# Second-layer softmax: the reciprocal row sums go through DRAM and scale the head outputs, instead of scaling the probabilities

## Chip, cores and metric

The kernel runs on one core of one Trainium2 chip. The metric is device time in microseconds; smaller is better. Before the change the median of three runs is 756.14 us (754.92 to 758.21).

## The reference

Two layers over 512 latent tokens and 256 context tokens with 1024 features. The first layer uses differential attention, the second grouped-query attention with 8 query heads of 128, 2 key/value heads and a gate path. What matters here is the second layer's mixer:

```python
def sweep_attention(q, k, v):
    ...
        s = jnp.einsum('bqhgd,bkhd->bhgqk', qblk.astype(jnp.float32), k32) * scale
        p = jax.nn.softmax(s, axis=-1)
        return jnp.einsum('bhgqk,bkhd->bqhgd', p.astype(v.dtype), v)
    ...

def gqa_mixer(h, hc, w_in, w_out, qk_g, cos, sin, with_ctx_out):
    ...
    q, k, v, z = jnp.split(p, [GQ_Q_WIDTH, GQ_Q_WIDTH + GQ_KV_WIDTH, GQ_Q_WIDTH + 2 * GQ_KV_WIDTH], axis=-1)
    q = rms_norm(q.reshape(B, L, GQ_HEADS, GQ_HEAD_DIM), qk_g[0])
    ...
    def attend(qq, kk, vv, gate):
        o = sweep_attention(qq, kk, vv)
        o = o.reshape(o.shape[0], o.shape[1], BRANCH_WIDTH)
        return (o * jax.nn.silu(gate)) @ w_out
```

In the second layer only latent queries produce output; they read 512 latent and 256 context keys in one softmax, 768 in all.

## The kernel before

Everything is fp32 in and out. A matrix product is three TensorE matmuls on a high and a low half of each operand (type fp32r; a ScalarE cast makes the high half, a subtraction on VectorE or GpSimd the low half), so most operands appear as pairs in the profile: `whi`/`wlo` weights, `ah`/`al` probabilities, `vh`/`vl` values, `qh`/`ql`, `kh`/`kl`.

The stages are: the modulation vectors and norms, the first layer's projections and attention, its output projection, then the second layer's keys and values, its attention with the projections of q and of the gate z mixed in as filler for TensorE, and the output projection.

**The second layer's attention** goes over 8 heads and, in each, two halves (`ch`) of two query tiles of 128 rows. Such a pair of tiles is the unit of the work, 16 in all. For a tile (`unit` in `s1_units`, lines 2078 to 2109):

- TensorE writes the scores of 768 keys into a two-bank PSUM tile `sc`; VectorE reduces the negated row maximum; ScalarE scales it (`nmx`).
- ScalarE writes the exponentials into its half of the pair's tile `pp` and accumulates the row sum `l` (line 2103). VectorE takes its reciprocal (2104), and `scaled(EN1, ...)` multiplies the probabilities by it on GpSimd (2105).
- After the second tile `turn` (680 to 692) transposes the pair in 32 x 32 blocks on VectorE, stores it to a DRAM scratch tile `dr` and loads it back as `at` in four transfers, which completes the transposition. Both are issued on SP's queue, and the loads wait until the store has landed.

`pv1_steps` then takes the pair in three steps: ScalarE casts `ah` from `at`, VectorE subtracts for `al`, TensorE multiplies with the values into a bank `bk` (`pv_mm`). After the last step ScalarE copies the bank to the head's tile `g1` (line 2143), transposed: rows are the 128 features of the head, columns its queries. `heads_out` puts the columns back in order. When both halves of heads 0 to 6 are done, GpSimd multiplies the tile with the gate (`gate_mul1`); the last head takes `last_half` on VectorE for each half. `tail1` splits all heads for the output projection.

Other work of that stage: `q_proj` writes two heads of q for a token tile into a bank, and `rope_tok` (1932) reads it with VectorE (`ta`, `tb`) before GpSimd adds the parts; `z1_proj` makes the gate; weights come in as `raw` on SP's queue and are split by ScalarE and GpSimd or VectorE.

**What sets the order.** The kernel is run through twice. In the first pass the class `Plan` records each instruction with what it must wait for and prices it (`price`, 291): so many ns for an instruction by engine, shape and operand place, and a surcharge when VectorE and GpSimd are busy on SBUF data at once (`op.kind` at 340 to 342, used in `schedule`). `schedule` (345) runs all engines and SP's queue in a model with these prices; DMA landing times are in it by size (line 393). `plan` (447) repeats this 12 times with priorities from the latest allowed start, and then applies `MOVES` (101): each number seeds a random shift of the priorities of a few neighbouring instructions of one engine, in any stage (`shift`, 474). The second pass emits the program with the order of each engine, SP among them, fixed as planned. So an instruction stands in its engine's queue behind all that the plan put ahead of it, ready or not.

Of the kernel before, what the change touches and what calls it, by code (L numbers as in the profile page):

```python
# [9 lines left out]
F32 = mybir.dt.float32  # L10
# [6 lines left out]
P = 128  # L17
D = 1024
KT = 8
# [58 lines left out]
QTR = 2.0  # L78
EG0 = 'v'
EP0 = 'p'  # L80
EN1 = 'p'
ESW = 'v'
EG1 = 'a'
LM = (4.5, 4.5)
AB = 2
P0B = 2
# [1 line left out]
PPB = 2  # L88
DRSPLIT = 1
DRB = 6  # L90
PEWAY = ((), ())


def f32(ap):
# [3 lines left out]


RANKP = ("PE",)  # L100
MOVES = (121443151, 661718012, 381041855, 51234840, 372779023, 957281565, 227970257, 105033711, 68446900, 773563299,
# [22 lines left out]
SLACK = 0  # L124


# [22 lines left out]
class Plan:  # L149


    def __init__(self, mem, psum, drams, sizes):
        self.mem, self.drams, self.sizes, self.turns = mem, drams, sizes, 0
        self.psum = dict(psum)
        self.banks = {t.tensor.name: t.free_size() for t in psum.values()}
        self.width = mem.shape[1]
        self.ops, self.offs, self.tail, self.seen = [], [0], None, {}
        self.marks = []
        self.pools, self.stack = [], {"left": [], "right": []}
        for q in QUEUE:  # L160
            setattr(self, q, Queue(self.add, QUEUE[q]))
# [3 lines left out]
        return Pool(self, name, side, psum)  # L165

    def scratch(self):
        self.tile = lambda *args, **kw: self.dram()
        return nullcontext(self)

    def dram(self):
        self.turns += 1
        return self.drams[(self.turns - 1) % len(self.drams)]


    @contextmanager
# [39 lines left out]
    def add(self, q, meth, args, kw):  # L216
# [14 lines left out]
        for aps_, w in ((ins, 0), (outs, 1)):  # L231
            for ap in aps_:
                far = ap.space == bass.MemoryType.DRAM
                if far and all(ap.tensor.name != d.tensor.name for d in self.drams):
                    continue
                name, spans, parts = (ap.tensor.name, [(0, 2048)], 1) if far else self.places(ap)
                if name not in self.banks and not far:
                    at = spans[0][0]
                    p = next(p for p in self.pools if p.open and p.base <= at < p.base + p.size)
                    p.users.add(op)  # L240
                    if p.mark is not None:
                        op.preds.add(p.mark)
                    held = p.held[max(lo for lo in p.held if lo <= at)]
                    ring = held[0]
                    held[2].add(op)
                    op.preds |= held[3]
                    if held[1] is None:
                        held[1] = len(ring)
                        ring.append(op)
                    if held[1] and ring[held[1] - 1] is not op:  # L250
                        op.soft.add(ring[held[1] - 1])
# [39 lines left out]
    def price(self, op, outs, ins):  # L291
# [47 lines left out]
                op.cost = 190 + 2.155 * n  # L339
        if q in ("DVE", "POOL") and op.kind is None and op.meth not in ("reciprocal", "tensor_reduce", "memset"):  # L340
            if not any(ps) and outs[0].tensor.name not in self.banks:
                op.kind = 0.75 if n <= 8 else 0.5 if sum(free_size(a) > 8 for a in ins) >= 2 else 0.25


    def schedule(self, rank):
# [15 lines left out]
        while len(order) < count:  # L361
# [28 lines left out]
            elif op.kind == "D":  # L390
                s = max(s, land.pop(0))
                go = s + (450 if op.cost == 131072 else 480 if op.cost == 196608 else 440)
                rate, base = {196608: (207, 1450), 786432: (420, 900), 131072: (350, 2500)}.get(op.cost, (350, 1450))
                dma = max(dma, go + 300) + op.cost / rate
                end = dma + base - 300 + DPAD
                land.append(end)
# [199 lines left out]
def tile_backbone(  # L596
# [83 lines left out]
    def turn(pool, pp, w=384):  # L680
        flat = pp.rearrange("p b u x -> p (b u x)")
        nc.vector.transpose(flat, flat)
        at = pool.tile([P, 4, w], F32, tag=f"at{w}", name=nm("at"), bufs=ATB if w == 384 else 1)
        for lo in range(0, 4, 4 // DRSPLIT):
            n = 4 // DRSPLIT
            dr = drp.tile([P // DRSPLIT, 4 * 384], F32, tag="dr", name=nm("dr"), bufs=DRB)[:, :4 * w]
            nc.sync.dma_start(dr, flat[32 * lo:32 * (lo + n), :])
            for a in range(4):
                nc.sync.dma_start(
                    at[32 * a:32 * a + 32, lo:lo + n, :],  # L690
                    dr.rearrange("(q j) (a c) -> a j q c", j=32, c=w)[a])
        return at

    def dma_way(layer, h, ch):
        return (h, ch) not in PEWAY[layer]
# [1221 lines left out]
    with pl.pool("t1", "right") as t1p:  # L1917
        gT1 = [None] * KT
        ropeb = con.tile([P, 2, 512], F32, tag="rope", name="ropeb")
        nc.scalar.dma_start(ropeb, rope_b)  # L1920
        gq = t1p.tile([P, 2, P], F32, name="gq")
        nc.scalar.dma_start(gq, b_qk_g.partition_broadcast(P))
        cosb = ropeb[:, 0, :].rearrange("p (t d) -> p t d", t=4)
        sinb = ropeb[:, 1, :].rearrange("p (t d) -> p t d", t=4)
# [132 lines left out]
        def z1_proj(h):  # L2057
# [13 lines left out]
            szt1[h] = sz  # L2071
            gate_mul1(h)

        def s1_units(h, ms):
            res, pair = [], {}
            moved = dma_way(1, h, ms[0] // 2)

            def unit(m):
# [20 lines left out]
                else:  # L2099
                    pt = unit_row(pair[0], m % 2)  # L2100
                    pv_, src = pt.rearrange("p (j n) -> p j n", j=2), scv
                l = small()
                nc.scalar.activation(pv_, src, AF.Exp, scale=sr, bias=nmx, accum_out=l)
                nc.vector.reciprocal(l, l)
                scaled(EN1, pt, pt, l)
                if not moved:
                    res.append(pt)
                elif m % 2:
                    res.append(turn(t1q, pair[0]))

            return res, [Step(lambda m=m: unit(m), 0.97) for m in ms]

        def pv1_steps(h, at, ch, after, ts, ms):
# [19 lines left out]
            def mstep(kt):  # L2133
# [6 lines left out]
                if kt == 4:  # L2140
                    if ch == 0:
                        gT1[h] = t1p.tile([P, 512], F32, tag="g1", name=nm("g1"), bufs=8)
                    (nc.scalar.copy if EG1 == "a" else nc.vector.tensor_copy)(*heads_out(gT1[h][:, ch * 256:ch * 256 + 256], o, moved))
                    close(o)
                    if ch == 1 and h < KT - 1:
                        done1.add(h)
                        gate_mul1(h)
                    elif ch == 1:
                        last_half(1)
# [231 lines left out]
```

## Time and profile before

| | |
|---|---|
| Runs | 754.92, 758.21, 756.14 us |
| Profiled execution, its own time | 757.93 us |
| Its span, first to last instruction | 755.8 us |
| Mean granted TensorE clock | 0.996 |
| Probability tiles in the second layer's attention | 557.7 to 706.3 us of the span |

Times in the profile count from the first instruction. A row of a group gives engine, operation, output and inputs by tile name, shapes, count, then busy us, mean ns of one, and the idle time of the engine just before them with what ended it. A row of a window gives for each engine its busy time and, in brackets, its instructions. A wait row reads: engine and tile, who released it, us in total, times, longest. PEld is the weight load of TensorE, which runs beside its matmuls; SPq is the queue that issues most transfers. All instructions have line 509 in the rows, since one helper records them; tiles tell them apart.

### The profile page before, as it was taken

What the parts mean: (1) busy time and instruction counts of PE and PEld (TensorE: products, weight loads), DVE (VectorE), ACT (ScalarE), POOL (GpSimd) and SP (SyncE); (2) the same over time, 40 slices, a digit from 0 to 9 for tenths busy, and PEclk for the clock granted to TensorE, in tenths of its full rate; (3) what the DMA queues carried; (4) which work ended last, traced back from release to release, by engine and by line L of the source; (5) the groups of instructions that cost most, each with busy time, mean ns of one, the idle gap of its engine ahead of it and who ended that gap; (6) DMA issues with size and microseconds to landing.
All of it is one profiled execution on the core that took longest, in us unless ns stands there. A gap on an engine that the chain in (4) does not pass through costs nothing. (4 is left out here: it accounts for less than half of the span.)

```text
span 755.8 us, 13984 instructions
## 1 busy us (share of the span) xinstructions
PE 733.9 (97%) x5046; PEld 654.3 (87%) x5046; DVE 567.1 (75%) x881; ACT 480.0 (64%) x1085; POOL 466.7 (62%) x512
## 2 busy tenths in 40 slices
PE   7999999999999999899999999999999989999996
PEld 6788888888878898797989998899999988888986
DVE  4445899988988869787889844789547787799744
ACT  6544477767676646666569853784476776678741
POOL 5463787885795738747755412467779887674201
PEclk9999999999999999999999999999999999999999
DMA  9933263647474655835666182034436785888613
GB/s 347 405 123 124 95 198 109 188 164 223 140 221 142 212 165 176 255 100 172 229 171 179 31 307 84 2 97 157 145 117 190 224 257 163 232 239 266 165 46 111
DMA packets 51444, 131.75 MB, mean 174 GB/s; under 512 B 6448, under 2 KB 27184, under 8 KB 49840
## 3 DMA queue, kind: packets, MB, share of 16 engines
q1 hardware_dynamic: 47952, 125.73, 52.7%
q10 hardware_dynamic: 3424, 5.15, 2.1%
q8 instruction: 39, 0.64, 0.4%
q14 instruction: 29, 0.24, 0.1%
HBM read 97.56 MB, written 29.10 MB: 168 GB/s over the span
## 5 line engine op out<-in xcount | busy, mean ns | idle before, releaser
L509 PE MATMUL bk<-whi,h 128*128 128x256 f32 (+1 forms) x1184 | 244.0, 298 | 2.9 <-DVE tb L509 1.8
L509 PE MATMUL bk<-h,whi 128*128 128x512 f32 (+2 forms) x832 | 222.4, 348 | 0.1
L509 POOL TENSOR_TENSOR wlo<-raw,whi 128x256 fp32r<-128x256 f32 x200 | 171.1, 879 | 56.1 <-ACT whi L509 53.7
L509 PEld LDWEIGHTS bk<-whi,h 128*128 128x128 f32 x1184 | 189.6, 189 | 13.9 <-issue 2.9
L509 PE MATMUL bk<-wlo,h 128*128 128x256 f32 (+1 forms) x592 | 172.3, 298 | 0.0
L509 PEld LDWEIGHTS bk<-h,whi 128*128 128x128 f32 x832 | 144.4, 188 | 15.6 <-issue 2.8
L509 PE MATMUL bk<-h,wlo 128*128 128x512 f32 (+2 forms) x416 | 144.0, 348 | 0.0
L509 POOL TENSOR_SCALAR pp<-pp,sm 128x768 f32<-128x768 f32 (+1 forms) x78 | 82.0, 1054 | 68.0 <-DVE sm L509 58.4
L509 PEld LDWEIGHTS bk<-wlo,h 128*128 128x128 f32 x592 | 109.8, 188 | 4.9 <-issue 1.6
L509 DVE TENSOR_REDUCE sm<-sc 128x1 f32<-128x768 f32 (+2 forms) x114 | 101.0, 893 | 14.7 <-PE sc L509 14.5
L509 DVE TENSOR_TENSOR al<-at,ah 128x512 fp32r<-128x512 f32 x103 | 98.7, 978 | 13.7 <-ACT ah L509 9.9
L509 ACT CAST whi<-raw 128x1024 fp32r<-128x1024 f32 (+1 forms) x70 | 71.5, 1023 | 27.1 <-PE bk L509 14.9
L509 PEld LDWEIGHTS bk<-h,wlo 128*128 128x128 f32 x416 | 78.3, 188 | 8.7 <-issue 2.4
L509 ACT CAST ah<-at 128x512 fp32r<-128x512 f32 x103 | 61.7, 618 | 33.3 <-PE bk L509 21.0
L509 DVE STREAM_TRANSPOSE pp<-pp 128x1536 f32<-128x1536 f32 (+1 forms) x39 | 61.4, 1577 | 5.7 <-POOL pp L509 5.6
L509 DVE SCALAR_TENSOR_TENSOR pp<-p,sm,pp 128x768 f32<-128x768 f32 (+1 forms) x46 | 55.8, 1219 | 4.4 <-POOL pp L509 2.8
L509 PE MATMUL sc<-qk,qk 64*128 64x384 f32 (+1 forms) x480 | 50.7, 341 | 0.4 <-DVE qk L509 0.4
L509 ACT ACTIVATE jk<-bk 128x128 f32<-128x128 f32 (+4 forms) x66 | 22.7, 345 | 41.8 <-PE bk L509 22.8
L509 ACT ACTIVATE pp<-sc,sm 128x768 f32<-128x768 f32 (+1 forms) x46 | 35.4, 770 | 21.5 <-DVE sm L509 20.8
L509 PEld LDWEIGHTS sc<-qk,qk 64*128 64x128 f32 x480 | 38.3, 184 | 10.7 <-issue 3.5
L509 POOL TENSOR_TENSOR sz<-sz,za 128x384 f32<-128x384 f32 (+1 forms) x24 | 28.3, 1180 | 23.8 <-ACT za L509 23.8
L509 ACT ACTIVATE za<-za 128x384 f32<-128x384 f32 (+1 forms) x72 | 40.0, 559 | 4.7 <-DVE za L509 4.1
(206 smaller groups left out, 1365.1 us busy)
## 6 DMA issues: line engine op xcount, KB each, us to landing
dr<-pp SPq DMA_DIRECT2D x32, 768.0 KB, 4.0
at<-dr SPq DMA_DIRECT2D x128, 192.0 KB, 4.3
raw<-in_a_w SPq DMA_DIRECT2D x30, 512.0 KB, 3.9
araw<-in_ada_g SPq DMA_DIRECT2D x12, 1024.0 KB, 7.0
raw<-in_b_w SPq DMA_DIRECT2D x20, 512.0 KB, 3.8
ag<-in_ada_s SPq DMA_DIRECT2D x16, 512.0 KB, 9.9
raw<-in_w_out SPq DMA_DIRECT2D x16, 512.0 KB, 4.5
sw<-qr ACTq DMA_DIRECT2D x32, 128.0 KB, 2.1
```

The source lines that it names most:

```text
L509: self.ops.append(getattr(eng, meth)(*args, **kw))
```

## The change

The second layer's probabilities are no longer multiplied by the reciprocal row sums. The sums of a pair's two tiles go side by side into one small tile; after the pair's transpose one reciprocal is taken for both, and a new function `spread` stores the 256 values to a DRAM row `rw` and loads that row back to all 128 partitions as `rl`. Since a head's output has queries along its columns, `rl` scales it directly. For heads 0 to 6 ScalarE's copy stays and GpSimd multiplies the copy in place; for the last head VectorE multiplies out of PSUM, in place of the copy.

```diff
+    def spread(dst, cols):
+        n = dst.shape[-1]
+        rw = drp.tile([1, T], F32, tag="rw", name=nm("rw"), bufs=RWB)[0, :n]
+        nc.sync.dma_start(rw.rearrange("(u p) -> p u", p=P), cols)
+        nc.sync.dma_start(dst, rw.partition_broadcast(P))
...
-        gq = t1p.tile([P, 2, P], F32, name="gq")
+        gq = t1p.tile([P, 2, P], F32, tag="gq", name="gq", bufs=2)
...
-                l = small()
-                nc.scalar.activation(pv_, src, AF.Exp, scale=sr, bias=nmx, accum_out=l)
-                nc.vector.reciprocal(l, l)
-                scaled(EN1, pt, pt, l)
+                if m % 2 == 0:
+                    pair[1] = small(2)
+                l = pair[1]
+                nc.scalar.activation(pv_, src, AF.Exp, scale=sr, bias=nmx, accum_out=l[:, m % 2:m % 2 + 1])
                 if not moved:
                     res.append(pt)
                 elif m % 2:
                     res.append(turn(t1q, pair[0]))
+                if m % 2:
+                    nc.vector.reciprocal(l, l)
+                    rls[h, m // 2] = t1p.tile([P, 256], F32, tag="gq", name=nm("rl"), bufs=2)
+                    spread(rls[h, m // 2], l)
...
-                    (nc.scalar.copy if EG1 == "a" else nc.vector.tensor_copy)(*heads_out(gT1[h][:, ch * 256:ch * 256 + 256], o, moved))
+                    gs, rl = gT1[h][:, ch * 256:ch * 256 + 256], rls.pop((h, ch))
+                    if h < KT - 1:
+                        nc.scalar.copy(*heads_out(gs, o, moved))
+                        nc.gpsimd.tensor_tensor(gs, gs, rl, ALU.mult)
+                    else:
+                        nc.vector.tensor_tensor(*heads_out(gs, o, moved), heads_out(rl, o, moved)[0], ALU.mult)
                     close(o)
```

The tiles `rl` use two buffers, which they share with the norm weights `gq` of the stage before. The DRAM rows `rw` have four (`RWB = 4`).

The planner changes with it. It knows the second kind of DRAM scratch, and keeps the stores to one kind of scratch in their recorded order. Two prices change, and the list of moves is replaced, from 230 numbers to 93, so that every engine's order is drawn anew in both layers:

```diff
-                op.kind = 0.75 if n <= 8 else 0.5 if sum(free_size(a) > 8 for a in ins) >= 2 else 0.25
+                op.kind = 0.75 if n <= 8 else 0.5 if sum(free_size(a) > 8 for a in ins) >= 2 else 0.6 if q == "POOL" else 0.25
...
-                rate, base = {196608: (207, 1450), 786432: (420, 900), 131072: (350, 2500)}.get(op.cost, (350, 1450))
+                rate, base = {196608: (207, 1450), 786432: (420, 900), 131072: (350, 1500), 1048576: (300, 2400)}.get(op.cost, (350, 1450))
...
-MOVES = (121443151, 661718012, 381041855, 51234840, 372779023, 957281565, 227970257, 105033711, 68446900, 773563299,
...
+MOVES = (981570915, 14270391, 906039641, 558903032, 215614573, 493334795, 311902228, 1040721268, 1036705418, 226433417,
...
```

More of the change, by code (lines that the diff above doesn't have):

```diff
@@ L80 @@
 EP0 = 'p'
-EN1 = 'p'
 ESW = 'v'
-EG1 = 'a'
 LM = (4.5, 4.5)
@@ L90 @@
 DRB = 6
+RWB = 4
 PEWAY = ((), ())
@@ L149, with __init__ @@
 class Plan:
-    def __init__(self, mem, psum, drams, sizes):
-        self.mem, self.drams, self.sizes, self.turns = mem, drams, sizes, 0
+    def __init__(self, mem, psum, scratches, sizes):
+        self.mem, self.sizes = mem, sizes
+        self.scratches = {tag: list(ring) for tag, ring in scratches.items()}
+        self.stores = {}
+        self.drams = {t.tensor.name for ring in scratches.values() for t in ring}
         self.psum = dict(psum)
@@ L167, in scratch, with dram @@
     def scratch(self):
-        self.tile = lambda *args, **kw: self.dram()
+        self.tile = lambda *args, **kw: self.dram(kw["tag"])
         return nullcontext(self)
-    def dram(self):
-        self.turns += 1
-        return self.drams[(self.turns - 1) % len(self.drams)]
+    def dram(self, tag):
+        ring = self.scratches[tag]
+        ring.append(ring.pop(0))
+        return ring[-1]
     @contextmanager
@@ L233, in add @@
                 far = ap.space == bass.MemoryType.DRAM
-                if far and all(ap.tensor.name != d.tensor.name for d in self.drams):
+                if far and ap.tensor.name not in self.drams:
                     continue
                 name, spans, parts = (ap.tensor.name, [(0, 2048)], 1) if far else self.places(ap)
+                if far and w:
+                    if name[:2] in self.stores:
+                        op.soft.add(self.stores[name[:2]])
+                    self.stores[name[:2]] = op
                 if name not in self.banks and not far:
@@ L2072, in z1_proj @@
             gate_mul1(h)
+        rls = {}
         def s1_units(h, ms):
@@ L2367 @@
             mem = mp.tile([P, MEM // 4], F32, name="mem")[:]
-            drams = [drp.tile([P // DRSPLIT, 4 * 384], F32, name=f"dr{i}")[:, :] for i in range(DRB)]
+            scratches = {
+                "dr": [drp.tile([P // DRSPLIT, 4 * 384], F32, name=f"dr{i}")[:, :] for i in range(DRB)],
+                "rw": [drp.tile([1, T], F32, name=f"rw{i}")[:, :] for i in range(RWB)],
+            }
             sizes, pl = None, None
             while pl is None or sizes != pl.sizes:
-                pl = Plan(mem, psum, drams, sizes)
+                pl = Plan(mem, psum, scratches, sizes)
                 tile_backbone(pl, *args)
```

31 rows, old and new, of the table MOVES are left out of this document.

## The prediction

> **What bounds the kernel now.** I read the page first, then windows by stage, then the waits of TensorE in the second layer, then the timeline around the largest of them, and last the tiles that the change touches.
>
> ```profile
> span 755.8 us, 13984 instructions
> PE 733.9 (97%) x5046; PEld 654.3 (87%) x5046; DVE 567.1 (75%) x881; ACT 480.0 (64%) x1085; POOL 466.7 (62%) x512
> ```
>
> TensorE is busy for 733.9 of 755.8 us. The change removes no matmul, so it can only win back idle TensorE time, or time at a low clock. The windows show where that lies (columns: PE, PEld, DVE, ACT, POOL busy us, granted clock, DMA share, GB/s).
>
> ```profile
> 12.00:110.00 98.00, 96.47 (x670) 78.64 (x669) 60.21 (x97) 50.49 (x93) 60.01 (x68) 1.00 0.57 204
> 110.00:440.00 330.00, 325.69 (x2308) 287.91 (x2307) 279.82 (x403) 226.01 (x482) 222.84 (x204) 1.00 0.56 171
> 440.00:556.00 116.00, 115.66 (x814) 107.32 (x813) 74.74 (x141) 66.19 (x199) 61.41 (x90) 1.00 0.37 125
> 556.00:600.00 44.00, 44.00 (x316) 42.35 (x315) 31.79 (x60) 29.88 (x81) 38.99 (x52) 1.00 0.58 175
> 600.00:700.00 100.00, 93.74 (x567) 84.78 (x566) 84.30 (x115) 75.65 (x166) 67.82 (x68) 0.98 0.80 233
> 700.00:747.60 47.60, 47.60 (x313) 43.38 (x312) 25.84 (x39) 22.96 (x52) 8.69 (x16) 1.00 0.31 91
> ```
>
> The second layer's attention runs from about 557 to 706 (rows of its probability tile are below). TensorE is full until 600 and again from 700. Between 600 and 700 it idles 6.26 us, with VectorE busy 84% and the DMA engines 80%. The first layer's attention (110 to 440) idles 4.31 us in a stretch three times as long. So 600 to 700 is where the changed code can gain. TensorE's own waits from 520 to 724 name the late parties:
>
> ```profile
> PE bk L509 <- DVE tb L509: 1.8, 1, 1.8
> PE bk L509 <- DVE al L509: 1.3, 2, 0.8
> PE bk L509 <- ACT ah L509: 1.2, 1, 1.2
> PE bk L509 <- ACT g L509: 0.9, 2, 0.5
> PE sc L509 <- ACT pp L509: 0.9, 2, 0.6
> ```
>
> They sum to 6.1 us, nearly all of the 6.26. Half of it is VectorE (`tb`, the rotary products of q; `al`, the low half of the probabilities). The longest wait is followed by a drop of the granted clock:
>
> ```profile
> 632.00:636.00 4.00, 4.00 (x22) 4.00 (x22) 2.40 (x6) 3.25 (x11) 3.07 (x3) 0.65 0.54 134
> 636.00:640.00 4.00, 4.00 (x28) 3.88 (x28) 2.73 (x8) 2.44 (x7) 2.60 (x4) 0.92 0.32 67
> ```
>
> At 0.65 and 0.92 of full speed these 8 us hold 4 x 0.35 + 4 x 0.08 = 1.7 us less of TensorE's work. What made VectorE late is in the timeline. First the two waits on TensorE, then VectorE before them:
>
> ```profile
> 622.31 0.50 PE L509 MATMUL bk<-al,vh 128*128 128x256 f32 x2 [0.84 <-DVE al L509]
> 631.80 0.36 PE L509 MATMUL bk<-whi,h 128*128 128x256 f32 x1 [1.80 <-DVE tb L509]
> ```
>
> ```profile
> 619.10 1.78 DVE L509 STREAM_TRANSPOSE pp<-pp 128x1536 f32<-128x1536 f32 x1 [0.74 <-POOL pp L509]
> 620.80 1.46 DVE L509 TENSOR_TENSOR al<-at,ah 128x512 fp32r<-128x512 f32 x1
> ...
> 627.58 1.78 DVE L509 STREAM_TRANSPOSE pp<-pp 128x1536 f32<-128x1536 f32 x1 [0.73 <-POOL pp L509]
> 629.28 0.92 DVE L509 TENSOR_REDUCE sm<-sc 128x1 f32<-128x768 f32 x1
> 630.84 0.42 DVE L509 TENSOR_TENSOR ta<-bk,ropeb 128x256 f32<-128x256 f32 x1 [0.63 <-ACT jk L509]
> 631.18 0.48 DVE L509 TENSOR_TENSOR tb<-bk,ropeb 128x128 f32<-128x128 f32 x2
> ```
>
> In both cases VectorE stands for 0.74 and 0.73 us in front of the 1.78 us transpose, because GpSimd's normalisation of the same tile (`POOL pp`) isn't done. Everything behind the transpose in VectorE's fixed order, `al` and `tb` among it, comes later by as much. That normalisation is what the change takes away.
>
> **The change part by part.** *Normalisation on GpSimd, removed.* The rows are those of the probability tile from 552 to 708 (min/median/max ns, first and last start; the last row is idle time before it, in us and times):
>
> ```profile
> L509 POOL TENSOR_SCALAR pp<-pp,sm x32: 900/915/2457, 557.7 to 703.1; 128x768 f32<-128x768 f32 x32
> L509 DVE STREAM_TRANSPOSE pp<-pp x16: 1759/1774/1780, 562.7 to 704.5; 128x1536 f32<-128x1536 f32 x16
> L509 SPq DMA_DIRECT2D dr<-pp x16: 326/338/375, 564.5 to 706.3; - x16
>   POOL pp L509: 5.6, 7
> ```
>
> 32 instructions of 0.90 to 2.46 us go. Each pair of query tiles loses one hop of at least 0.9 us between exponential and transpose, and VectorE loses 5.6 us of standing, in 7 places. The 16 transposes are (704.5 - 562.7) / 15 = 9.45 us apart: that is the period of a pair.
>
> *What is added on the engines.* The nearest rows, from 520 to the end:
>
> ```profile
> L509 DVE RECIPROCAL sm<-sm 128x1 f32<-128x1 f32 x32 | 4.8, 151 | 6.4 <-ACT pp L509 6.3
> L509 POOL TENSOR_TENSOR q<-ta,tb 128x256 f32<-128x256 f32 x16 | 12.7, 796 | 2.0 <-DVE tb L509 1.9
> L509 DVE TENSOR_TENSOR ta<-bk,ropeb 128x256 f32<-128x256 f32 x16 | 6.7, 417 | 9.3 <-ACT jk L509 9.3
> ```
>
> Seven heads get 14 GpSimd products of 128x256, at 0.796 us 11.1 us. GpSimd gave up at least 32 x 0.90 = 28.8 us, so its net load falls by at least 17.7 us. The products stand behind ScalarE's copy of a head and before the gate product on the same engine; TensorE's bank is freed by the copy, as before, so the product lies off its path. The last head has two products out of PSUM on VectorE in place of two ScalarE copies: 2 x 0.417 = 0.8 us. Reciprocals go from 32 to 16, -16 x 0.151 = -2.4 us. VectorE's work falls by 1.6 us in all.
>
> *What is added on SP's queue.* For each of 16 pairs there is one store of 256 sums from a [128, 2] tile and one load of them to all 128 partitions: 32 issues at 0.338 us, 10.8 us. The load waits until the store has landed. Queued behind it on SP are the next pair's `dr` store and `at` loads and the weight loads. SP's waits from 556 to 706:
>
> ```profile
> SPq L509 <- DMA dr<-pp: 36.0, 11, 5.8
> SPq L509 <- DVE pp L509: 26.6, 9, 7.4
> SPq L509 <- POOL wlo L509: 15.3, 7, 3.5
> SPq L509 <- DVE sm L509: 11.6, 6, 3.0
> ```
>
> SP already waits 36.0 us for `dr` stores to land before it may issue their `at` loads. If the sums are stored right behind `dr`, their landing hides in that wait, and the load costs only its issue. Besides, SP stands at least 26.6 + 15.3 + 11.6 = 53.5 us for engines, 3.3 us a pair, which hides the two issues (0.68 us). I cost this part at 1 us given back over the stage; its bounds are 0, if all is covered, and 22 us, the unhidden case below. I take the low end because a `dr` landing stands in front of nearly every load of a pair anyway.
>
> For the price of these transfers the trace has no like; the nearest (KB, us from issue to landing):
>
> ```profile
> subg<-in_a_sub SPq DMA_DIRECT2D x1, 0.5 KB, 6.9
> lamb<-in_a_lam SPq DMA_DIRECT2D x1, 128.0 KB, 8.1
> gq<-in_b_qk_g ACTq DMA_DIRECT2D x1, 128.0 KB, 2.9
> DMA to landing us min/median/max: 3.2/4.0/7.3
> ```
>
> The first is 128 words of four bytes, the second and third are rows spread to 128 partitions like the new load, and the fourth is the `dr` stores of 552 to 708. Store and load together take at least 2 x 2.9 = 5.8 and at most 6.9 + 8.1 = 15 us. They are needed only at the end of the pair's product with V:
>
> ```profile
> L509 ACT COPY g<-bk x16: 359/373/377, 581.1 to 721.2; 128x256 f32<-128x256 f32 x16
> ```
>
> That copy starts 581.1 - 562.7 = 18.4 us after the first pair's transpose and 721.2 - 704.5 = 16.7 after the last one's, so even 15 us is hidden. The two buffers for the spread sums cover the same stretch: a pair's buffer is wanted again 2 x 9.45 = 18.9 us after its transpose plus the landing of a store (3.2 at least), 22.1 us; it is free after copy and product, 18.4 + 0.37 + 0.80 = 19.6 us. The 2.5 us between them hide it; once GpSimd comes later than that, SP would stand by the excess.
>
> *The sum.* I take back whole the waits whose cause is VectorE, 1.8 + 1.3 = 3.1 us, and the clock drop that follows the longest, 1.7 us. Of the other 3.0 us (`ah`, `g`, `pp`) I take half, 1.5 us: they are late through the same chain of a pair, but some belong to ScalarE's own order. From these 6.3 us I give back 1 us for SP and 0.1 us for the slower last product (0.417 against 0.373 us), which leaves 5.2 us. The bounds are 0, if each wait returns elsewhere, and the whole 6.26 + 1.7 = 8.0 us. The profiled execution took 757.93 us, of which 755.8 are its span; it goes to 752.7. That execution is 1.8 us above the median of the runs, 756.14, so I forecast 751 us.
>
> *The orders drawn anew* touch every engine's order in both layers. Nothing in this trace shows the new one. I cost them at nothing, with bounds of 4 us each way from the 4.31 us that TensorE idles from 110 to 440: a better order can win that back at most, and I allow a worse one as much again.
>
> **The rivals.** *The waits only move.* TensorE's five late parties are three engines; with `al` and `tb` earlier, ScalarE's copies and casts come last at the same places, or the first layer's new order loses what the second gains. For it: only 3.1 of 6.1 us are VectorE's. Against it: in this stretch ScalarE has 24 us of 100 idle. The gain is then 0 to 2 us and the time about 755.
>
> *SP becomes the bound.* The place is the spread of the sums on SP. If the order puts the store of the sums behind the `at` loads, its landing no longer hides behind `dr`'s, and SP stands once more per pair. It has 3.3 us a pair to spare, of which the two issues take 0.68: beyond a landing of 2.6 us SP sets the period. At the median 4.0 us of a `dr` store each pair grows by 1.4 us, 22 us over 16 pairs; if a third of the pairs are ordered so, 7 us. The time would be 763 us. Against it: the transpose comes before the reciprocal in the code and both are short against a `dr` landing, so the two stores have good reason to stand together.
>
> The Trainium skill, page "DMA: Bandwidth & Descriptors", section "Rules for kernel authors", speaks against the change here: a transfer whose last dimension isn't contiguous becomes one descriptor for each element and should be rearranged. By it the store of the sums would be 256 descriptors of four bytes and would take longer than a store of its size. The trace doesn't bear this out where it can: 128 words of four bytes took 6.9 us while 128 KB in the same stage took 8.1; a store of this kind it doesn't show.
>
> **How the numbers follow.** Half a per cent, 3.8 us, is about what a measurement of this kernel can tell from no change, so faster means below 752.4 us and slower above 759.9. The forecast has a chance of 0.50: its gain of 5.2 us, with up to 8.0 + 4 us at its best, 744 us. That the waits only move has 0.32. SP as the bound, with a first layer made worse by the new order counted in it, has 0.18. The range goes from 744 to 761 us: it leaves out the upper part of the last case and little else. The forecast alone would lie between 744 and 753.
>
> **What would show it.** Right: no GpSimd instruction on `pp`, none of VectorE's transposes waiting for GpSimd, TensorE busy over 97 of 100 us in the second layer's attention, its granted clock 1.00 throughout, and SP's wait for the stores of sums small beside its wait for `dr`. Wrong: TensorE's idle time there unchanged with ScalarE's casts named as the late party; or SP waiting long for the sums and `ah` waiting for `at`; or more than 4 us of new idle time from 110 to 440, which would be the orders' doing.

## The result and the profile after

The kernel after takes 856.49 us in the median of four runs (853.0 to 862.76); before, measured beside it, 756.17 us. The ratio is 1.133, with a 95% interval of 1.1255 to 1.1411: 100 us slower, where 751 us was forecast. The profiled execution took 862.76 us; its page says of the span and the engines:

```profile
span 861.0 us, 13979 instructions
PE 755.1 (88%) x5046; PEld 671.6 (78%) x5046; DVE 555.0 (64%) x867; ACT 480.4 (56%) x1083; POOL 442.1 (51%) x494
```

TensorE does the same 5046 matmuls. Of the 105.2 us by which the span grew, it is idle for 84.0 (105.9 against 21.9) and busy for 21.2 more, at a mean granted clock of 0.942 in place of 0.996. The windows of the kernel after, with the columns of before (the attention of the second layer now ends near 800):

```profile
12.00:110.00 98.00, 95.66 (x665) 77.90 (x663) 60.93 (x97) 51.01 (x94) 59.23 (x67) 1.00 0.55 196
110.00:440.00 330.00, 326.12 (x2297) 286.65 (x2297) 270.68 (x404) 225.32 (x479) 226.62 (x205) 1.00 0.57 177
440.00:556.00 116.00, 116.00 (x820) 107.90 (x819) 74.74 (x147) 64.87 (x196) 55.68 (x85) 1.00 0.33 111
556.00:600.00 44.00, 36.93 (x248) 35.59 (x247) 22.09 (x42) 24.84 (x68) 28.49 (x45) 0.88 0.58 141
600.00:700.00 100.00, 56.25 (x316) 52.88 (x314) 39.24 (x55) 37.56 (x85) 27.09 (x33) 0.76 0.70 129
700.00:820.00 120.00, 79.72 (x445) 71.05 (x444) 63.81 (x82) 58.82 (x119) 35.03 (x34) 0.83 0.74 144
```

Up to 556 us nothing happened: TensorE idles 6.2 us in the first three windows, as before. From 556 on everything is slower. TensorE has 56 of 100 us of work where it had 94, at a clock of 0.76, VectorE is busy 39 where it was 84, and the DMA share is still 0.70 while the rate fell from 233 to 129 GB/s: engines of the DMA that are counted as busy and move little. TensorE's waits from 520 to 830:

```profile
PE bk L503 <- ACT ah L503: 56.3, 7, 12.6
PE sc L503 <- ACT pp L503: 34.7, 4, 15.1
```

ScalarE is only the last link. Its own waits from 556 to 830 name transfers of the probabilities, a load (`at`) and a store (`dr`, which must have left `pp` before the next exponentials may go in):

```profile
ACT ah L503 <- DMA at<-dr: 61.7, 8, 13.1
ACT pp L503 <- DMA dr<-pp: 34.9, 5, 16.7
```

SP's queue, which issues these, waits in the same stretch for three things:

```profile
SPq L503 <- DMA dr<-pp: 66.3, 11, 10.6
SPq L503 <- POOL g L503: 50.6, 7, 13.3
SPq L503 <- DMA rw<-sm: 37.3, 9, 10.3
```

Before it was 36.0 us for `dr`, 0.4 for GpSimd's `g`, and there were no sums to wait for. The new transfers explain the second and third row, but not the first: why should the old store land later? The DMA issues from 552 to 830 (KB each, median us to landing of those whose landing the profile gives) show it:

```profile
dr<-pp SPq DMA_DIRECT2D x16, 768.0 KB, 12.6
...
rl<-rw SPq DMA_DIRECT2D x16, 128.0 KB, 7.0
...
rw<-sm SPq DMA_DIRECT2D x16, 1.0 KB, 11.5
```

A `dr` store took 4.0 us before and takes 12.6 now, and 1 KB takes 11.5. SP's timeline at the first pair, first after, then before:

```profile
564.38 0.33 SPq L503 DMA_DIRECT2D dr<-pp  x1
566.02 0.38 SPq L503 DMA_DIRECT2D rw<-sm  x1
577.05 1.75 SPq L503 DMA_DIRECT2D at<-dr  x4
578.90 0.38 SPq L503 DMA_DIRECT2D rl<-rw  x1
```

```profile
564.53 0.33 SPq L509 DMA_DIRECT2D dr<-pp  x1
568.54 1.75 SPq L509 DMA_DIRECT2D at<-dr  x4
```

In this pair the store of the sums stands right behind `dr`, as the prediction wanted. Yet the `at` loads start 12.7 us after `dr` instead of 4.0. What the DMA engines do in these 16 us (564 to 580, 40 slices of 0.4 us; tenths busy, then GB/s):

```profile
DMA  0029989630090000000000000020000000039999
GB/s 21 0 41 461 384 369 415 231 33 15 31 15 0 0 0 0 0 0 0 0 0 0 0 0 0 0 15 0 0 0 0 0 0 0 0 61 307 338 238 184
```

The 768 KB go out within 3 us, then the words; from 568.8 on the engines show next to nothing for some 9 us, until `dr` and `rw` are both reported as landed. So the time isn't spent on moving data. In later pairs other transfers are on the way too, and some of them trickle through such a gap: in the same view from 632 to 648 the engines move 0 to 92 GB/s from 639.2 to 646.8.

Not every pair has this order. Counted in the order of issue, the sums of the second, ninth and tenth pair go out only behind their own pair's `at` loads, and in five other pairs a load `rl` stands between `dr` and the sums. SP's timeline at the tenth and eleventh pair, whose stores of sums go out together with that of the ninth:

```profile
706.47 0.33 SPq L503 DMA_DIRECT2D dr<-pp  x1
712.87 1.91 SPq L503 DMA_DIRECT2D at<-dr  x4
714.91 0.35 SPq L503 DMA_DIRECT2D dr<-pp  x1
...
716.54 3.32 SPq L503 DMA_DIRECT2D rw<-sm  x3
```

### The profile page after: what moved, and what is told of

It reads as the page before. It is cut to its first block, busy times and chain, and to the rows that moved or that the text cites. A ratio compares the mean times of both kernels' runs of the same rounds, so it can differ in the third digit from the quotient of the medians.

```text
span 861.0 us, 13979 instructions
## 1 busy us (share of the span) xinstructions
PE 755.1 (88%) x5046; PEld 671.6 (78%) x5046; DVE 555.0 (64%) x867; ACT 480.4 (56%) x1083; POOL 442.1 (51%) x494
## 4 chain that ended last, share of the span: by engine, by line
PE 59%; DMA 23%; DVE 5%; POOL 4%; ACT 4%; issue 3%; SPq 1%; ACTq 0%; DVEq 0%; POOLq 0%
PE bk L503 48%; PE sc L503 11%; DMA dr<-pp 8%; DMA at<-dr 7%; DMA rw<-sm 4%; DMA sw<-qr 2%; DVE al L503 2%; DVE pp L503 1%; DMA raw<-in_w_out 1%; POOL qk L503 1%; SPq L503 1%; ACT pp L503 1%; POOL qr L503 1%; POOL wlo L503 1%; DVE sm L503 1%
## 5 line engine op out<-in xcount | busy, mean ns | idle before, releaser
L503 PE MATMUL bk<-h,whi 128*128 128x512 f32 (+2 forms) x832 | 228.2, 353 | 0.0
L503 POOL TENSOR_TENSOR wlo<-raw,whi 128x256 fp32r<-128x256 f32 x200 | 167.6, 863 | 92.6 <-ACT whi L503 89.4
L503 PEld LDWEIGHTS bk<-h,whi 128*128 128x128 f32 x832 | 146.6, 191 | 17.2 <-issue 4.7
L503 DVE TENSOR_TENSOR al<-at,ah 128x512 fp32r<-128x512 f32 x103 | 94.4, 931 | 97.5 <-ACT ah L503 86.8
L503 PE MATMUL bk<-ah,vh 128*128 128x256 f32 x96 | 24.5, 342 | 56.3 <-ACT ah L503 56.3
L503 PEld LDWEIGHTS bk<-ah,vh 128*128 128x128 f32 x96 | 19.5, 239 | 59.1 <-ACT ah L503 58.5
L503 POOL TENSOR_SCALAR pp<-pp,sm 128x768 f32<-128x768 f32 (+1 forms) x46 | 42.3, 924 | 33.5 <-DVE sm L503 14.2
L503 PE MATMUL sc<-kh,qh 128*128 128x384 f32 x64 | 24.2, 379 | 34.8 <-ACT pp L503 34.7
L503 ACT ACTIVATE pp<-sc,sm,qrs 128x768 f32<-128x768 f32 x32 | 31.7, 990 | 35.4 <-DMA dr<-pp 34.9
```

Of the source, the lines that this page charges most:

```text
L503: self.ops.append(getattr(eng, meth)(*args, **kw))
```

## The experiments

Two theories came first. A: the price is that of the store of 256 single words. B: it is that of the round through DRAM on SP's queue, whatever its store looks like. Before, measured beside the runs, was 755.7 to 757.1 us. Where no interval is given, one execution was measured.

**The words alone (e1).** The kernel before, in its own order, with this added behind each `dr` store (shortened; the two values of a pair also lie side by side in one small tile now, and nobody reads the row):

```diff
+                if m % 2:
+                    rw = drp.tile([1, T], F32, tag="rw", bufs=4)[0, :256]
+                    nc.sync.dma_start(rw.rearrange("(u p) -> p u", p=P), pair[1])
```

> The kernel before in its own order, probabilities still normalised, with one thing added: behind each of the 16 stores of a probability pair, a store of the pair's 256 sums to DRAM as 256 words of four bytes, which nothing reads. Theory A (the word store stops the transfer engines for several us and all else follows): the dr stores of the second layer land in 9 to 13 us instead of 4.0, the pairs run late by 4 to 6 us each, and the time is 800 to 860 us. Theory B (the store is cheap; the new order, the two rl buffers and the extra waits on SP make the loss): 755 to 760 us, dr landing 4 to 5 us.

Measured: 832.74 us, ratio 1.1016 (1.0975 to 1.1057). 16 stores of 1 KB that nobody waits for cost 77 us. DMA issues of this run from 552 to 800 and a wait of SP from 556 to 800:

```profile
dr<-pp SPq DMA_DIRECT2D x16, 768.0 KB, 11.2
```

```profile
SPq L509 <- DMA dr<-pp: 127.4, 16, 14.5
```

The stores of `dr` are as late as in the kernel after. Theory A holds for most of the loss.

**One row in place of words, control (e7).** The same as e1, but the 1 KB comes as one row from the rope table: `dma_start(rw.unsqueeze(0), ropeb[0:1, 0, :256])`.

> The kernel before in its own order, with 16 stores of one row of 1 KB from another tile behind the dr stores: the control of e1, same number of stores and bytes, one piece each. If the words are what costs, 755 to 760 us and dr landing at 4 us; if a further store on this queue costs by itself, 800 us or more.

Measured: 755.69 us. Neither the issue, nor the bytes, nor one more landing costs anything.

**One row in the kernel after (e2).** `spread` in the recorded order, but its store is that row, so the head outputs are scaled by other numbers.

> The changed kernel with the same order, but the store of sums replaced at its place by one row of 1 KB from another tile, so the head outputs are scaled by other numbers. Everything else of the change stays: loads of rl, their wait for the store, two buffers, products, new orders. Theory A: landing of the store 2 to 3 us, dr landing back at 4 us, time 747 to 760 us. Theory B: 840 us or more, SP still waiting tens of us for GpSimd's g.

Measured: 798.24 us, ratio 1.0548 (1.0513 to 1.0582). 58 us less, but still 42 above before and outside the 747 to 760 us of theory A, so there is a second cause. SP's waits from 556 to 760 name it:

```profile
SPq L503 <- POOL g L503: 60.8, 9, 11.8
SPq L503 <- DMA dr<-pp: 29.9, 8, 7.7
```

The wait for `dr` is back to the level of before (36.0). The largest wait is now for GpSimd's product: SP stands at a load `rl`, because GpSimd has not yet used the buffer of two pairs earlier, and behind that load stand the next `dr`, `at` and weights.

**Runs of 128 bytes (e3) and of 8 bytes (e4).** In e3 the reciprocals are spread over 32 columns and transposed in 32 x 32 blocks on VectorE, so that eight runs of 32 words, two from each of four partitions, go out; the small-tile ring goes from 24 to 22 for the space:

```diff
-                    nc.vector.reciprocal(l, l)
+                    lt = t1q.tile([P, 64], F32, tag="lt", name=nm("lt"), bufs=1)
+                    nc.vector.reciprocal(lt.rearrange("p (u x) -> p u x", u=2), l.unsqueeze(2).to_broadcast([P, 2, 32]))
+                    nc.vector.transpose(lt, lt)
...
-        nc.sync.dma_start(rw.rearrange("(u p) -> p u", p=P), cols)
+        nc.sync.dma_start(rw.rearrange("(u a j) -> a u j", u=2, a=4), cols.rearrange("a (u j) -> a u j", u=2))
```

In e4 the row is ordered `(p u)`, so that each partition stores its two words as 8 bytes, and the products read it in that order.

> The changed kernel with the sums laid out on chip first: the reciprocal is spread over 32 columns, VectorE transposes 32 by 32 blocks, and the store moves 8 runs of 128 bytes instead of 256 words; order planned anew from the same moves; one ring of small tiles shortened from 24 to 22 to make room. Theory A: store landing 2 to 3 us and a time of 748 to 762 us, about as e2. Theory B: 830 us or more.

> The changed kernel with the DRAM row in the order of the sums tile, so that the store is 128 pieces of eight bytes; the products read rl with a stride. If the stop goes by the number of pieces, it halves: store landing 6 to 8 us, time 790 to 820 us. If it is a fixed price of a store with small pieces, nothing changes: 850 us. Theory B: 850 us too.

Measured: e3 789.39 us, ratio 1.0444 (1.0415 to 1.0472); e4 817.52. Half as many pieces twice as long take away 39 of the 67 us that runs of 128 bytes take away. e3 too misses the range of theory A (748 to 762 us). SP's waits in e3, 556 to 760:

```profile
SPq L503 <- POOL g L503: 47.0, 10, 8.8
SPq L503 <- DMA dr<-pp: 26.0, 11, 5.4
SPq L503 <- DMA rw<-lt: 15.2, 8, 4.8
```

One such wait for `g` shows what GpSimd is doing meanwhile, first GpSimd, then SP:

```profile
604.72 2.10 POOL L503 TENSOR_TENSOR wlo<-raw,whi 128x256 fp32r<-128x256 f32 x3 [9.05 <-ACT whi L503]
606.78 0.72 POOL L503 TENSOR_TENSOR g<-g,rl 128x256 f32<-128x256 f32 x1
```

```profile
596.71 2.13 SPq L503 DMA_DIRECT2D at<-dr  x4
607.53 0.34 SPq L503 DMA_DIRECT2D rl<-rw  x1
```

GpSimd isn't busy: its first product stands in its fixed order behind weight splits, which stand 9.05 us for ScalarE's half of them. SP issues the next `rl` as soon as the product is done, 8.7 us after it had finished with the `at` loads.

**Four buffers (e5).** e3 with four tiles `rl` in place of two, and the ring of the queries' tiles (`qt`) cut from ten to eight for the space.

> e3 with four buffers for rl instead of two; to make room the ring of q and k tiles goes from 10 to 8. Theory C (two buffers: SP stands at the load of rl until GpSimd has used the tile of two pairs earlier, and dr stores, at loads and weights stand behind it): SP's wait for GpSimd's g falls from 47 us to under 10, TensorE's idle time from 600 to 700 from 17 us to under 9, time 750 to 765 us. Theory D (the loads of rl take the transfer engines' time, or the new order is bad by itself): 780 us or more.

Measured: 762.89 us, ratio 1.0093 (1.0068 to 1.0118), 26.5 less than e3. SP has no wait for `POOL g` left, and TensorE has its work again from 600 to 700:

```profile
600.00:700.00 100.00, 97.15 (x592) 88.32 (x591) 88.62 (x115) 77.88 (x171) 48.67 (x56) 0.98 0.83 248
```

So the loss of 100 us is 67 for the words (856.5 to 789.4) and 26.5 for the two buffers; 6.7 us are left. e3 and e5 each come with an order drawn anew, which by itself moves such a kernel by up to 9 us (below), so the parts are no more exact than that. e2, in the order of the kernel after, divides the loss into 58 for the words and 42 for all else.

**No load (e6).** e3 without `rl`: the head outputs are multiplied by a constant tile.

> e3 without the loads of rl: sums are laid out and stored in 8 runs as in e3, and the products use a constant tile in place of rl, so the head outputs are scaled by other numbers. Theory C: no wait of SP for GpSimd's g, 747 to 760 us, which is what taking the normalisation off GpSimd is worth once transfers cost nothing. Theory D with a bad order: still 775 us or more.

Measured: 752.89 us, ratio 0.9959 (0.9936 to 0.9981). This is what unnormalised probabilities give without the loads, 3 us, in the order that this list of moves gives.

**Where words disturb (e8, e10, e11).** e1 again with the words 512 bytes (e8) or 64 bytes (e10) apart in DRAM, where the row `rw` grows with the distance, and with neighbouring words that come from one partition (e11); shortened:

```diff
-                    nc.sync.dma_start(rw.rearrange("(u p) -> p u", p=P), pair[1])
+                    nc.sync.dma_start(rw.rearrange("(u p x) -> p u x", p=P, x=128)[:, :, 0], pair[1])  # e8; e10 has x=16
+                    nc.sync.dma_start(rw.unsqueeze(0), ropeb[0:1, 0, 0:512:2])  # e11
```

> e1 with the 256 words 512 bytes apart in DRAM instead of side by side. If the stop comes from neighbouring words being written by different engines to the same piece of memory, store landing falls to 2 to 4 us and the time to 755 to 770 us. If each small write has its price wherever it goes, as e1: landing 10 us or more, 820 to 840 us.

> e1 with the words 64 bytes apart in DRAM, between e1 (4 bytes, 833 us, landing 12.7 us) and e8 (512 bytes, 756 us, 4.0 us). If words disturb each other only inside 64 bytes: landing 4 us, 755 to 760 us. If inside 512 bytes: 8 words share such a piece instead of 128, landing 5 to 12 us, 765 to 830 us.

> e1 with the 256 words taken from every second word of one partition instead of two from each of 128, to the same neighbouring places in DRAM. Same number of pieces and the same addresses; consecutive words now go to one transfer engine (16 each) or all to one. If it matters which engines write neighbouring words, landing falls below 8 us and the time under 790 us; if the address alone matters, 820 us or more.

Measured: e8 755.8 us, e10 760.19, e11 848.09. e10 is 2 us above the highest of the 13 runs of before beside it, 758.2 (beside e5 to e8 one reached 760.93); its clock was 0.97 from 12 to 110 us, ahead of the first word, so I don't put this down to the words. DMA issues of e8 from 552 to 708 and of e10 from 552 to 720, then e11's store of the row, issue to landing:

```profile
dr<-pp SPq DMA_DIRECT2D x16, 768.0 KB, 4.1
...
rw<-sm SPq DMA_DIRECT2D x16, 1.0 KB, 4.0
```

```profile
dr<-pp SPq DMA_DIRECT2D x16, 768.0 KB, 4.3
...
rw<-sm SPq DMA_DIRECT2D x16, 1.0 KB, 4.0
```

```profile
DMA to landing us min/median/max: 8.7/13.6/20.0
```

256 words from 128 partitions land in 4.0 us when they lie 64 bytes or more apart, and the time stays within some 4 us of before; 256 neighbouring words cost 92 us even from one partition. So the price lies in single words to neighbouring places in DRAM, not in the number of words (e8, e10), nor in where they come from (e11), nor in the 1 KB as such, which costs nothing in one piece (e7).

**A plan that knows the price (e12).** The planner is told that 1 KB holds the transfer engines for some 6 us more.

> The changed kernel, word stores included, with the planner told that a store of 1 KB holds the transfer engines for 6 us, in place of 3 ns at its general rate. If an order drawn for the true price could hide the stop: under 800 us. If 16 stops of about 8 us on a queue that every pair needs can't be hidden by order: 830 us or more.

Measured: 862.25 us. This order doesn't hide the store. In the planner's model the price delays the store itself and the transfers behind it, but not the `dr` in front, so whether an order that knows this could do better is not shown.

**The remainder, and the orders.** e9 is e5 with the layout made in the first 64 columns of the tile that later takes the loaded row, which gives the small tiles their ring of 24 back. In e13 the sums go straight to columns 0 and 32 there (GpSimd fills the 64 columns with ones first), so that the reciprocal is one of 128x2:

```diff
-                    pair[1] = small(2)
-                l = pair[1]
+                    rls[h, m // 2] = t1p.tile([P, 256], F32, tag="gq", name=nm("rl"), bufs=4)
+                    lt = rls[h, m // 2][:, :64]
+                    nc.gpsimd.memset(lt, 1.0)
+                lt = rls[h, m // 2][:, :64]
+                l = lt[:, 0:64:32]
...
+                    nc.vector.transpose(lt, lt)
+                    spread(rls[h, m // 2], lt[0:P:32, :])
```

e14 and e15 are e13 with the list of moves of the kernel before and with none (`MOVES = ()`); e16 and e18 are e9 with the same two; e17 is the kernel before with none.

> e5 with the layout of the sums done in the first columns of the rl tile itself, so that the single layout buffer is gone, for which VectorE waited in e3 and e5 until the store had landed (10.7 us in e3, 4.2 in e5); the ring of small tiles is back at 24. If that wait is what keeps e5 7 us above the kernel before: 750 to 757 us. If it is the plan, drawn anew with each such change: 757 to 768 us, with the difference spread over the first layer too.

> The kernel after with the sums written straight into columns 0 and 32 of the first 64 columns of the tile that later takes the loaded row (GpSimd sets these 64 columns to one first), a reciprocal of 128x2, the 128x64 transpose on VectorE, eight runs of 128 B as the store, four such tiles and eight of the queries' ring. Theory 'layout' (the 5 us between the run without loads, 752.9 us, and the run with the layout in the loaded tile, 758.5 us, are VectorE's: 16 reciprocals of 128x64 at 0.53 us against 128x2 at about 0.15): 753 to 755 us. Theory 'loads' (they are the loads' share of the transfers and of SP): 757 to 760 us. Theory 'order' (they are the order that the list of moves gives, which was drawn for another kernel): anything from 752 to 762, and the next two runs differ from this one by 3 us or more.

> The same kernel with the order drawn from the list of moves of the kernel before. Theory 'order': differs from the run with the new list by 3 us or more. Theories 'layout' and 'loads': within 2 us of it.

> The same kernel with no list of moves, so with the order that the planner gives by itself. Theory 'order': 5 to 25 us above the run with the new list, nearly all of it in the first layer too, since no list was drawn for it. Theories 'layout' and 'loads': within 2 us of it.

> The run with the layout in the loaded tile (758.5 us with the new list of moves) with the list of the kernel before. Theory 'order': differs by 3 us or more from 758.5. Theories 'layout' and 'loads': 757 to 760 us.

> The kernel before with no list of moves, so with the planner's own order; nothing else changed. It says what the change is worth when neither kernel has an order drawn for it: the repaired change without a list took 756.2 us. Theory 'the change is worth something once its spread is repaired' (the forecast's 5.2 us, and 3 us by the run without loads): 759 to 775 us. Theory 'the change is worth nothing, the order makes all the difference': 754 to 758 us.

> The layout in the loaded tile, reciprocal of 128x64, with no list of moves; with the new list it took 758.5 us and with the old list 767.6. Theory 'order': another value again, anywhere from 755 to 770, and its difference from the small layout without a list (756.2 us) has another sign than under the new list (-4.9 us) or the old one (+6.7 us). Theory 'layout' (the larger reciprocal costs 16 x 0.38 = 6 us of VectorE): 759 to 762 us.

Measured, in us, with the ratio to before's own list, in three sets whose kernel before took 756.0 to 757.1 us:

| kernel | list of after | list of before | no list |
|---|---|---|---|
| before | – | 756 | e17 761.29 (1.0062 to 1.0096) |
| e9, reciprocal 128x64 | e9 758.46 (0.9999 to 1.0051) | e16 767.63 (1.0112 to 1.0174) | e18 763.59 (1.0075 to 1.0119) |
| e13, reciprocal 128x2 | e13 763.35 (1.006 to 1.0122) | e14 760.96 (1.0037 to 1.0074) | e15 756.2 (0.9973 to 1.0017) |

One and the same kernel spreads over 7 us in the last line and over 9 in the line above it, by the list alone. The two reciprocals, grouped by line (busy us, mean ns), are those of e9 and of e13:

```profile
L503 DVE RECIPROCAL rl<-sm 128x64 f32<-128x64 f32 x16 | 8.3, 531 | 0.0
```

```profile
L503 DVE RECIPROCAL rl<-rl 128x2 f32<-128x2 f32 x16 | 2.2, 150 | 0.0
```

The smaller one saves VectorE 6.1 us, and the time falls by 6.7 and 7.4 us under two lists and rises by 4.9 under the third. So the order matters by as much as was supposed, though not as was supposed in each run: e13 lies 1.4 us above its range, e14 only 2.4 us from e13, and e15 7 us below e13, where 5 to 25 above had been expected. The theory of the layout is not decided, and the sign of a difference of 5 us in this kernel can't be put down to the edit. Without lists the repaired change is 5.1 us faster than before in one form (e15, 756.2 against 761.3; 6.4 by the two ratios) and 2.3 us slower in the other (e18, 763.6); with each kernel's best list found here they are equal. No version with the whole computation beats the kernel before; whether e13 would with a list drawn for it is open, and wasn't tried.

## Why the prediction was wrong

**The step that failed** is "What is added on SP's queue", taken at 1 us with bounds of 0 and 22. It failed in two places.

*"If the sums are stored right behind `dr`, their landing hides in that wait, and the load costs only its issue."* In the kernel after not every pair has the order supposed. In e1 every pair has it, in 14 of 16 the store less than 1 us behind `dr`, and there it shows that the store of words isn't a guest behind `dr`: it keeps `dr` itself from landing, 11.2 us in place of 4.0 (12.6 in the kernel after). By e1 that alone is 77 us, by the way from after to e3 67, by e2 58. The price was taken from `subg`, 6.9 us, "128 words of four bytes": that is a load, which reads neighbouring words from DRAM and writes them apart, while the new transfer is a store to neighbouring words. The trace had no such store, and a row with the direction turned round was no bound for it: store and load took 11.5 + 7.0 us where 15 was the upper end. Even so the larger error was to price the transfer by itself and not by what it does to the one in front.

*"The 2.5 us between them hide it; once GpSimd comes later than that, SP would stand by the excess."* It came later: SP stands 50.6 us in the kernel after and still 47.0 in e3, where the words are gone, and two more buffers give 26.5 us. The product takes place when GpSimd's fixed order has it, not right behind the copy: in e3 the first copy starts at 582.5 and the first product at 606.8. The excess goes to everything behind on SP. The condition was right, and its cost, nothing, was wrong.

A part of this could be read from the kernel before. The 2.5 us come from the first and the last pair and from the mean period; in between the pairs are uneven. The rows of before for the 13th transpose, the 15th, and the 13th copy:

```profile
677.96 1.77 DVE L509 STREAM_TRANSPOSE pp<-pp 128x1536 f32<-128x1536 f32 x1
690.66 1.76 DVE L509 STREAM_TRANSPOSE pp<-pp 128x1536 f32<-128x1536 f32 x1
702.88 0.36 ACT L509 COPY g<-bk 128x256 f32<-128x256 f32 x1
```

By the prediction's own working this pair's buffer is wanted again at 690.66 + 3.2 = 693.9 us and free at 702.88 + 0.36 + 0.80 = 704.0, ten us too late before GpSimd adds any delay.

**The rule against the change.** The Trainium skill, page "DMA: Bandwidth & Descriptors", section "Rules for kernel authors", which spoke against the change, gave the right direction, and the prediction's sentence that the trace doesn't bear it out was wrong. Its reason is not what costs here: e8 and e10 have as many pieces of four bytes as e1, and their stores land in 4.0 us. Nor does the Trainium skill's section "Specifications" on the same page, by which pieces below 512 bytes are read, changed and written back, tell them apart, since the pieces are below 512 bytes in all three; in e3, with pieces of 128 bytes, `dr` lands after 5.4 us in the median. The measurement decides: words that are neighbours in DRAM cost, the same words 64 bytes apart don't.

**The rival "SP becomes the bound"** had the place, and the signs written down for it came: SP waits 37.3 us for the sums and `ah` 61.7 us for `at`. But its mechanism was a store behind the `at` loads in a third of the pairs, at 4.0 us each, for 763 us. That order did come, in three of 16 pairs, but it isn't what costs: e1 has it in none and loses 77 us. The loss is fourteen times as large as the rival's.

**What was right.** *GpSimd's normalisation:* no GpSimd instruction is left on `pp`, and VectorE's transposes wait for ScalarE alone. The probability tile after, 552 to 830, with the idle time before its instructions below:

```profile
L503 DVE STREAM_TRANSPOSE pp<-pp x16: 1761/1774/1780, 562.6 to 776.6; 128x1536 f32<-128x1536 f32 x16
...
  ACT pp L503: 2.8, 6
```

*The added work on the engines:* products of 0.80 us were expected on GpSimd, and of 0.417 on VectorE for the last head. The tile `rl` after:

```profile
L503 POOL TENSOR_TENSOR g<-g,rl x14: 721/740/1201, 604.1 to 799.9; 128x256 f32<-128x256 f32 x14
L503 DVE TENSOR_TENSOR g<-bk,rl x2: 424/424/424, 804.4 to 819.9; 128x256 f32<-128x256 f32 x2
```

*The gain in TensorE's waits,* 6.3 us: it can't be seen under the loss. e6 shows 3 us, e15 against e17 5.1, and e18 against e17 a loss of 2.3, so runs this close don't fix its size. In e6 TensorE is busy for 96.51 of the 100 us (93.74 before), at a clock of 1.00, and `al` and `tb` are still the late parties, 2.1 and 1.4 us: nearly half of the idle time and the clock drop came back, and the rest stayed. "The waits only move" is right by that rest. The stage itself did get faster, without much use: in e15 the 16 transposes of `pp` run from 564.2 to 693.6, 8.63 us a pair, and in e18 8.77, in place of 9.45 in before and 9.46 in e17. Yet e18 is slower than e17. TensorE was busy for 97% of the span before, so I take it that what the attention no longer covers is done after it; no run separates this.

*The orders drawn anew,* nothing within 4 us: TensorE idles 3.9 us from 110 to 440 in place of 4.3. For the kernel as it is, that is right; the lists tried later move the same kernel by 7 to 9 us, which is about the width of these bounds.

## What to carry to other kernels

Price a new transfer by what it does to the transfers around it and by its direction; where the trace has no store of that shape, leave the upper bound open or lay the data out on an engine first (here 0.53 or 0.15 us for the reciprocal and 0.23 for a transpose of 128x64, for runs of 128 bytes). A broadcast load on the queue that feeds the critical path needs a buffer that is surely free when its turn comes, since whatever stands behind it waits as well. In a kernel with a searched order, compare an edit under several orders before believing a difference of half a per cent.

## What the hardware showed that was not expected

- A store of 256 neighbouring words of four bytes lands after 12.7 us in the median of e1 and 13.6 in e11; the same words 64 or 512 bytes apart land after 4.0. Pieces of 8 bytes lie between (817.5 us for the kernel, against 856.5 and 789.4). Distances from 8 to 64 bytes were not tried.
- It holds up a store of 768 KB that was issued before it on the same queue (`dr` 4.0 to 11.2 us in e1), and loads issued behind it land late too (`at` in e1 5.6 us in the median and 13.7 at most, against 4.2 and 7.4). At the first pair of the kernel after, with little else on the way, the 16 engines show next to no packets for some 9 us; in e1's first pair their share is 0.00 from 568 to 574. What they wait for in that time the trace doesn't show, and it stays open.
- TensorE's clock went to 0.76 in the stretch where it was idle for 44 of 100 us, and the same matmuls took 21 us longer over the span.
